# The first norm of blocks 2 and 3 taken from x by features, in a stick-breaking attention layer

## The chip, the cores and the metric

One Trainium2 chip, and one of its cores: TensorE (PE in the profile, its weight loads PEld), VectorE (DVE), ScalarE (ACT), GpSimd (POOL), and the DMA queue that SyncE (SP) issues. The metric is the device time of one execution in microseconds. It is given as the median of several runs, and less is better.

## The reference, cut to what matters

One encoder layer on 2048 tokens of 1024 features, all float32: adaptive norm, stick-breaking attention with 16 heads, a gated residual, then a second norm and a dense SwiGLU. The change touches the first line alone.

```python
h = modulate(rms_norm(x, norm_g[i, 0]), sh_m, sc_m)   # h * (1 + scale) + shift, per feature
y = stick_breaking_mixer(h, sb_w_qkv[r], sb_w_o[r])   # qkv = h @ w_qkv, blocks of causal attention, @ w_o
x = x + gt_m * rms_norm(y, norm_g[i, 1])
h = modulate(rms_norm(x, norm_g[i, 2]), sh_f, sc_f)
x = x + gt_f * rms_norm(swiglu_ffn(h, ffn_w_in[i], ffn_w_out[i]), norm_g[i, 3])

def rms_norm(x, g):                                   # over the 1024 features of a token
    return x * lax.rsqrt(jnp.mean(x * x, axis=-1, keepdims=True) + EPS) * g
```

## The kernel before, in words

The tokens are cut into four blocks of 512 (numbered 0 to 3), the features into eight tiles of 128 (k = 0 to 7), the heads into eight pairs (p). Products want h with the features on the partitions: per tile, 128 x 512. A product in full precision is made of three matmuls with high and low halves (`mm3`, L172 to L176), so each tile of h is kept as a high half in fp32r and a low half that is the rest. These are the tiles `ht`.

The order on TensorE, ScalarE, VectorE and GpSimd is the order in which the code is written (a manual schedule; SP's order alone is chosen by the scheduler). Each of these queues works strictly in that order, so an instruction that waits holds up everything behind it.

`project` (L446) makes K, then Q, then V of one pair and block, eight k-steps each. They are called t = 1, 0 and 2, and their accumulators in PSUM `pj`. As pair 0 works on block b - 1, the first norm of block b (`nb` in the code) is put between its k-steps, at places that are written as (t, k). Attention units (scores `z`, sigmoids, the scan `w`, the product `a`, turns `t`, halves `aT`, the weighing `o`) are interleaved with these steps from the V product of block 1 on.

Before the change the first norm is done in two ways:

- Blocks 1 and 3 "by features" (`BY_FEATURES`, L73): x is loaded twice, by tokens (`x`, four tiles of 128 x 1024) for the sums of squares, and by features (`xc`, four tiles with two k each) for the values. ScalarE squares each token tile with a running sum (L165), VectorE and GpSimd make 1/rms of it (L167, L169), VectorE spreads it over 128 columns (L340), TensorE turns the four spread pieces into a row over all 512 tokens (`xr`, L352), ScalarE copies that to SBUF. VectorE (even k) or GpSimd (odd k) then multiply the feature tiles by this row (L372, L376); ScalarE makes the high half (L389, or L394 and L395), VectorE or GpSimd the low one (L390, L397).
- Block 2 by tokens: x is loaded once; after the same sums VectorE scales the token tiles (L338), and TensorE turns each k with four transposes (`xT`, L361). ScalarE applies gain and shift as it reads PSUM (`hf`, L383), VectorE makes both halves (L384, L385).

`NORM_AT` (L75) places the tiles k = 0, 1, 2 of the next block inside the V product before it; the tiles k = 3 to 7 are made inside the K product that uses them, at its k-steps 0 to 4.

Of the kernel before, what the change touches and what calls it, by code (L numbers as in the profile page):

```python
# [9 lines left out]
F32 = mybir.dt.float32  # L10
# [59 lines left out]

H2_STEP = 3

BY_FEATURES = (1, 3)  # L73

NORM_AT = [(2, 2), (2, 4), (2, 6)]  # L75

# [26 lines left out]
def hybrid_trunk_kernel(  # L103
# [183 lines left out]


    x_tiles, x_norm, x_rstd, x_cols, x_row = {}, {}, {}, {}, {}

    x_places = {}

    def x_place(b):
        if b not in x_places:
            x_places[b] = [
                att.tile([P, 2, D], F32, name=f"x{b}_{i}", tag="qt", bufs=BUFS["qt"]) for i in range(2)
            ]
        return x_places[b]

    def x_load(b, *which):  # L300
        for i in which or range(4):
            r0 = b * BT + i * P
            if b == 2:
                tok = x_place(b)[i // 2][:, i % 2]
            else:
                tok = att.tile([P, D], F32, name=f"x{b}_{i}", tag="v", bufs=BUFS["v"])
            nc.sync.dma_start(tok, x[r0 : r0 + P])
            x_tiles[b, i] = tok

    def cols_load(b, *which):  # L310
        for m in which or range(KC // 2):
            cols = att.tile([P, 2, BT], F32, name=f"xc{b}_{m}", tag="kt", bufs=BUFS["kt"])
            nc.sync.dma_start(cols, xt[b // 2, :, 2 * m : 2 * m + 2])
            x_cols[b, 2 * m], x_cols[b, 2 * m + 1] = cols[:, 0], cols[:, 1]

    def x_square(b, i):
        if b > 0:
            tok = x_tiles[b, i]
            if b in BY_FEATURES:
                junk = tok  # L320
            else:
                junk = att.tile([P, D], F32, name=f"xj{b}_{i}", tag="wraw", bufs=BUFS["wraw"])
            x_rstd[b, i] = rms_scale(att, tok, f"n0_{b}_{i}", junk=junk)
            return
        xn = att.tile([P, D], F32, name=f"xn{b}_{i}", tag="kt", bufs=BUFS["kt"])
        x_norm[b, i] = xn
        x_rstd[b, i] = rms_scale(att, x_tiles[b, i], f"n0_{b}_{i}", junk=xn)

    def x_scale(b, i):
        nc.vector.tensor_scalar(  # L330
            x_norm[b, i], x_tiles.pop((b, i)), x_rstd.pop((b, i)), None, op0=ALU.mult
        )

    def x_spread(b, i):

        if b not in BY_FEATURES:
            tok = x_norm[b, i] = x_tiles.pop((b, i))
            nc.vector.tensor_scalar(tok, tok, x_rstd.pop((b, i)), None, op0=ALU.mult)  # L338
            return
        nc.vector.tensor_scalar(  # L340
            x_tiles[b, i][:, :P], ones, x_rstd.pop((b, i)), None, op0=ALU.mult
        )

    def x_share(b):

        if b not in BY_FEATURES:
            return
        pool, tag = (tps, "t") if b < 2 else (accps, "acc")
        pt = pool.tile([P, BT], F32, name=f"xr{b}", tag=tag)
        for i in range(4):  # L350
            tok = x_tiles.pop((b, i))
            nc.tensor.transpose(pt[:, i * P : (i + 1) * P], tok[:, :P], ident)  # L352
        x_row[b] = tok[:, BT:]
        nc.scalar.copy(x_row[b], pt)

    def x_turn(b, k):

        pool, tag = (tps, "t") if b == 0 else (accps, "acc")
        pt = pool.tile([P, BT], F32, name=f"xT{b}_{k}", tag=tag)
        for i in range(4):  # L360
            nc.tensor.transpose(  # L361
                pt[:, i * P : (i + 1) * P], x_norm[b, i][:, k * P : (k + 1) * P], ident
            )
        return pt

    def scale_cols(b, k):

        if b not in BY_FEATURES:
            return
        u = x_cols[b, k]  # L370
        if k % 2 == 0 or b == 1:
            nc.vector.scalar_tensor_tensor(  # L372
                u, u, g_eff[:, 0, k : k + 1], x_row[b], op0=ALU.mult, op1=ALU.mult
            )
        else:
            nc.gpsimd.tensor_tensor(u, u, x_row[b], op=ALU.mult)  # L376

    def modulate(hl, b, k):

        gain, add = g_eff[:, 0, k : k + 1], mod[:, 0, k : k + 1]  # L380
        if b not in BY_FEATURES:
# [4 lines left out]
            return  # L386
        u = x_cols.pop((b, k))
        if k % 2 == 0 or b == 1:
            nc.scalar.activation(hl[:, 0], u, AF.Identity, bias=add)  # L389
# [56 lines left out]
    def project(at):  # L446
# [10 lines left out]
        def product(t):  # L457
# [7 lines left out]
            for k in range(KC):  # L465
                if t == 1:
                    if p == 0:
                        first_norm(b, k + (4 if b == 1 else 3))
                    if k == 0 and nb == 3:
                        cols_load(3)  # L470
                    if k in (3, 5) and waiting:
                        waiting.pop(0)()
                if nb == 2 and (t, k) == (0, 0):
                    x_load(3)
                square_at = {2: 0, 3: 1}.get(nb)
                if t == square_at and k < 4:
# [12 lines left out]
                yield  # L489
# [260 lines left out]
            )  # L750

    def turn_x(m):
        turned_x[m] = x_turn(0, m)

    def full(m):
        t = att.tile([P, BT], F32, name=f"hf0_{m}", tag="tmp", bufs=BUFS["tmp"])
# [26 lines left out]
    nc.sync.dma_start(c_act, c)  # L783
    row_load(0)
    nc.sync.dma_start(c_line[0:1], c_row)
    x_load(0)
    nc.sync.dma_start(b_cols, ada_b_cols)
    nc.sync.dma_start(gc, g_cols)
    row_load(1)
# [21 lines left out]
    row_done(0)  # L811
    for i in range(1, 4):
        x_square(0, i)
        x_scale(0, i - 1)
    for half in range(2):
        nc.scalar.copy(c_rows[:, half * BT : (half + 1) * BT], c_spread[half])
    x_scale(0, 3)
    row_load(6)
    row_load(7)
    first_acc = {  # L820
# [44 lines left out]
    low(2)  # L865
    products(1, 0, 2)
    products(1, 1, 2)
    for m in range(3):
        cols_load(1, m)
    store(0)  # L870
    x_load(1, 0, 1, 2)
    row_done(3)
    full(3)
    high(3)
# [24 lines left out]
    products(0, 4)  # L899
    products(1, 4)  # L900
    turn_x(7)
    x_place(2)
    store(2)
    x_load(2)
    cols_load(1, 3)
    full(6)
    high(6)
# [2 lines left out]
    row_done(7)  # L910
    low(6)
    x_square(1, 0)
    products(0, 5)
    products(1, 5)
    full(7)
# [842 lines left out]
```

## Time and profile before

| | us |
|---|---|
| median of 3 runs (lowest, highest) | 2849.67 (2843.75, 2851.95) |
| the profiled execution's own time | 2845.32 |
| its span in the trace | 2843.2 |
| TensorE busy in it | 2800.4 (98%) |
| VectorE, ScalarE, GpSimd busy | 2021.7, 1634.1, 1282.5 |

TensorE is busy in nearly all of the span. What it waits for is small and lies mostly in the first 150 us, where the first norm, the first projections and the first attention units of pair 0 run together. A timeline row gives the start in us from the span's start, the busy time, the engine, the line, the operation, and in brackets how long the engine sat idle before and what ended that. Rows of matmuls overlap: a 128x512 matmul is busy for 0.39 us, and the next one starts 0.23 us after it.

### The profile page before, as it was taken

To read this page: it belongs to the slowest core of one execution; us is meant where nothing else is said; L and a number is where in the kernel's file an instruction comes from. 1 tells how busy PE (TensorE), PEld (TensorE's weight loads), DVE (VectorE), ACT (ScalarE), POOL (GpSimd) and SP (SyncE) were. 2 spreads that over 40 slices of the span, in tenths; PEclk is the share of its full clock that TensorE was granted. 3 is DMA by queue.
4 is the path that set the end of the run, shared out by engine and by line. 5 is a ranking of instruction groups with operands and counts; after the bars stand their busy time and mean duration, and the time that the engine had idled before them with its cause. 6 is when DMAs were issued, how large, how long until landed. Compare 5 with 4: busy or idle time off the path is not lost.

```text
span 2843.2 us, 41829 instructions
## 1 busy us (share of the span) xinstructions
PE 2800.4 (98%) x13853; PEld 2338.5 (82%) x13853; DVE 2021.7 (71%) x2822; ACT 1634.1 (57%) x3274; POOL 1282.5 (45%) x2032
## 2 busy tenths in 40 slices
PE   9899999999999999999999999999999999999998
PEld 7788888888888888887888788888788888888887
DVE  6788888888888888888866766555775655134377
ACT  5787778787777877778645533333433333322243
POOL 0565666676576655666410122222222222544454
PEclk9999999999999999999999999999999999999999
DMA  9774556666665635546389644334453335545575
GB/s 368 285 230 157 186 170 212 211 188 216 196 217 177 218 116 175 193 136 228 97 293 317 196 139 153 120 103 160 127 176 110 112 105 166 191 138 153 181 227 187
DMA packets 239787, 521.05 MB, mean 183 GB/s; under 512 B 22481, under 2 KB 108497, under 8 KB 222674
## 3 DMA queue, kind: packets, MB, share of 16 engines
q1 hardware_dynamic: 239570, 518.38, 56.4%
q8 instruction: 109, 1.79, 0.3%
q14 instruction: 108, 0.88, 0.1%
HBM read 351.04 MB, written 118.49 MB: 165 GB/s over the span
## 4 chain that ended last, share of the span: by engine, by line
PE 84%; DVE 5%; DMA 5%; ACT 2%; issue 2%; POOL 1%; SPq 0%; DVEq 0%; POOLq 0%; ACTq 0%
PE s L174 9%; PE s L175 9%; PE s L176 9%; PE z L593 8%; PE o L672 8%; PE t L644 8%; PE pj L174 5%; PE pj L176 5%; PE pj L175 5%; PE o L176 4%; PE o L174 4%; PE o L175 4%; DMA h_s<-ht 1%; PE y L176 1%; PE y L174 1%
## 5 line engine op out<-in xcount | busy, mean ns | idle before, releaser
L634 POOL TENSOR_TENSOR a<-a,w 128x512 f32<-128x512 f32 (+3 forms) x640 | 621.6, 971 | 217.2 <-DVE w L627 130.3
L627 DVE TENSOR_TENSOR_SCAN w<-z,c,begin 128x512 f32<-128x512 f32 x384 | 489.3, 1278 | 83.9 <-ACT z L612 60.6
L174 PE MATMUL s<-r,l 128*128 128x512 f32 x1232 | 482.3, 391 | 5.1 <-DVE p L1490 3.9
L176 PE MATMUL s<-r,l 128*128 128x512 f32 x1232 | 480.2, 390 | 0.0
L175 PE MATMUL s<-r,l 128*128 128x512 f32 x1232 | 479.9, 390 | 0.0
L610 ACT ACTIVATE a<-z 128x512 f32<-128x512 f32 (+3 forms) x640 | 347.1, 542 | 170.4 <-PE z L593 137.6
L672 PE MATMUL o<-aT,v 128*128 128x512 f32 (+3 forms) x1280 | 385.0, 382 | 0.1
L660 DVE TENSOR_TENSOR aT<-t,aT 128x512 fp32r<-128x512 f32 (+3 forms) x640 | 358.6, 594 | 23.9 <-ACT aT L654 23.4
L593 PE MATMUL z<-kt,qt 128*128 128x512 f32 (+3 forms) x1280 | 363.7, 365 | 0.0
L654 ACT CAST aT<-t 128x512 fp32r<-128x512 f32 (+3 forms) x640 | 313.9, 533 | 73.5 <-PE t L644 63.4
L612 ACT ACTIVATE z<-z 128x512 f32<-128x512 f32 (+3 forms) x640 | 344.8, 539 | 0.0
L1498 POOL TENSOR_TENSOR one<-p,p 128x512 f32<-128x512 f32 x44 | 70.9, 1612 | 579.1 <-issue 322.2
L174 PE MATMUL pj<-ht,w 128*128 128x512 f32 x768 | 308.4, 402 | 4.3 <-issue 1.4
L644 PE MATMUL t<-begin,a 128*128 128x128 f32 x2176 | 295.7, 274 | 13.8 <-DVE aT L660 12.5
L644 PEld LDWEIGHTS t<-begin,a 128*128 128x128 f32 x2176 | 255.7, 141 | 64.1 <-DVE aT L660 14.0
L175 PE MATMUL pj<-ht,w 128*128 128x512 f32 x768 | 301.5, 393 | 2.0 <-DVE ht L390 1.5
L176 PE MATMUL pj<-ht,w 128*128 128x512 f32 x768 | 301.9, 393 | 0.0
L174 PEld LDWEIGHTS s<-r,l 128*128 128x128 f32 x1232 | 231.7, 188 | 56.0 <-ACT l L1351 2.9
L176 PEld LDWEIGHTS s<-r,l 128*128 128x128 f32 x1232 | 231.5, 188 | 48.3
L175 PEld LDWEIGHTS s<-r,l 128*128 128x128 f32 x1232 | 231.7, 188 | 48.0 <-issue 0.5
L622 DVE TENSOR_TENSOR_SCAN w<-z,begin 128x128 f32<-128x128 f32 (+3 forms) x256 | 208.6, 817 | 76.7 <-ACT z L612 67.5
L593 PEld LDWEIGHTS z<-kt,qt 128*128 128x128 f32 x1280 | 231.0, 189 | 37.6 <-DVE w L622 0.2
(178 smaller groups left out, 4879.3 us busy)
## 6 DMA issues: line engine op xcount, KB each, us to landing
ht<-h_s SPq DMA_DIRECT2D x108, 1024.0 KB, 8.2
wi<-in_win SPq DMA_DIRECT2D x86, 512.0 KB, 4.0
qt<-qn SPq DMA_DIRECT2D x124, 256.0 KB, 4.8
ol_qt<-act_s SPq DMA_DIRECT2D x56, 512.0 KB, 3.7
act_s<-S SPq DMA_DIRECT2D x66, 256.0 KB, 4.1
br<-in_wout SPq DMA_DIRECT2D x66, 256.0 KB, 3.5
h_s<-ht SPq DMA_DIRECT2D x16, 1024.0 KB, 9.8
o_s<-os SPq DMA_DIRECT2D x128, 128.0 KB, 2.6
```

Of the source, the lines that this page charges most:

```text
L174: nc.tensor.matmul(acc, lhs[0], rhs[0], start=first, stop=False, **kw)
L175: nc.tensor.matmul(acc, lhs[0], rhs[1], start=False, stop=False, **kw)
L176: nc.tensor.matmul(acc, lhs[1], rhs[0], start=False, stop=last, **kw)
L593: nc.tensor.matmul(z[:, :n], q[:, e, part, r * P : (r + 1) * P], k[:, e, :n], start=part == 0, stop=part == 1,)
L610: nc.scalar.activation(a[:, :n], z[:, :n], AF.Sigmoid, scale=QK_SCALE)
L612: nc.scalar.activation(z[:, :n], z[:, :n], AF.Sigmoid, scale=-QK_SCALE)
L627: nc.vector.tensor_tensor_scan(rest[:, rev], left[:, rev], begin[:, :BT][:, rev], initial=carries[r], op0=ALU.mult, op1=ALU.bypass,)
L634: nc.gpsimd.tensor_tensor(a[:, :n], a[:, :n], rest[:, 1 : n + 1], op=ALU.mult)
L644: nc.tensor.transpose(pt[:, rb * P : (rb + 1) * P], weighed[i, rb][:, j * P : (j + 1) * P], ident)
L654: nc.scalar.copy(hl[:, 0, t0:], pt[:, t0:])
L660: nc.vector.tensor_tensor(hl[:, 1, t0:], pt[:, t0:], f32(hl[:, 0, t0:]), op=ALU.subtract)
L672: nc.tensor.matmul(acc[:, t0:], lhs, hl[:, part, t0:], start=sc == qb and j == 0 and part == 0, stop=sc == 0 and j == 3 and part == 1,)
```

## The change

Blocks 1 to 3 are now all treated by features, and the token tiles of blocks 2 and 3 are no longer loaded.

- Sums of squares of blocks 2 and 3 come from the feature tiles: ScalarE squares each `xc` tile (two k, 1024 elements a partition) into `xs`; VectorE adds these to one tile, first by pairs of k (three additions of 1024 elements), then its two halves (512 elements). Four matmuls with a column of ones (`xq`, one column of output each) sum over the partitions, so 128 tokens land on the partitions of each column. VectorE and GpSimd make 1/rms for all four columns at once (`xm`, `xd`), VectorE spreads it into `xw`, and TensorE turns that into the row `xr`, which ScalarE copies to `xv`, as before for blocks 1 and 3.
- Block 2's squares use two tiles, so that ScalarE can fill one while VectorE adds the other. Block 3's four squares use one tile: the third and the fourth go to the half whose content VectorE has just added.
- Block 2 loses its 32 transposes, the scaling of its token tiles and `hf`; its odd k are multiplied on GpSimd and take two passes on ScalarE, as block 3's.
- The places are written in three tables: `XSQUARE_AT`, `XADD_AT` and `XSUM_AT` (for the summing matmuls, the spread and the turn). Each (t, k) stands before that k-step of the block before.
- The row and the spread pieces get tiles of their own in the pool "tmp". The constant `lead` holds -0.5 for the power.

```diff
-BY_FEATURES = (1, 3)
+XSQUARE_AT = {2: {(1, 2): 0, (1, 3): 1, (1, 6): 2, (1, 7): 3}, 3: {(1, 4): 0, (1, 5): 1, (0, 0): 2, (0, 2): 3}}
+XADD_AT = {2: {(1, 5): 1, (1, 7): 2, (0, 0): 3, (0, 1): 4}, 3: {(1, 7): 1, (0, 1): 2, (0, 3): 3, (0, 4): 4}}
+XSUM_AT = {2: [(0, 2), (0, 3), (0, 5)], 3: [(0, 5), (0, 6), (0, 7)]}
...
-    nc.vector.memset(lead, 0.0)
+    nc.vector.memset(lead, -0.5)
...
+    def cols_square(b, m):
+        if m == 0 or (m == 2 and b == 2):
+            both = att.tile([P, 2, 2, BT], F32, name=f"xs{b}_{m}", tag="qt", bufs=BUFS["qt"])
+            x_squares.setdefault(b, []).extend([both[:, 0], both[:, 1]])
+        elif m > 1 and b == 3:
+            x_squares[b].append(x_squares[b][1])
+        nc.scalar.activation(x_squares[b][m], x_pairs.pop((b, m)), AF.Square)
+
+    def cols_add(b, m):
+        total = x_squares[b][0]
+        if m < KC // 2:
+            nc.vector.tensor_tensor(total, total, x_squares[b][m], op=ALU.add)
+        else:
+            nc.vector.tensor_tensor(total[:, 0], total[:, 0], total[:, 1], op=ALU.add)
+
+    def cols_sum(b):
+        total = x_squares.pop(b)[0]
+        ps = accps.tile([P, BT], F32, name=f"xq{b}", tag="acc")
+        for i in range(4):
+            nc.tensor.matmul(
+                ps[:, i : i + 1], total[:, 0, i * P : (i + 1) * P], ones[:, 0:1], start=True, stop=True
+            )
...
+        nc.vector.tensor_scalar(ms, ps[:, :4], 1.0 / D, EPS, op0=ALU.mult, op1=ALU.add)
...
+        nc.gpsimd.tensor_tensor(rstd, ms, lead[:, :4], op=ALU.pow)
...
     def modulate(hl, b, k):
...
-        if b not in BY_FEATURES:
-            u = att.tile([P, BT], F32, name=f"hf{b}_{k}", tag="tmp", bufs=BUFS["tmp"])
-            nc.scalar.activation(u, x_turn(b, k), AF.Identity, bias=add, scale=gain)
-            nc.vector.tensor_copy(hl[:, 0], u)
-            nc.vector.tensor_tensor(hl[:, 1], u, f32(hl[:, 0]), op=ALU.subtract)
-            return
...
-                    if k == 0 and nb == 3:
-                        cols_load(3)
...
-                if nb == 2 and (t, k) == (0, 0):
-                    x_load(3)
-                square_at = {2: 0, 3: 1}.get(nb)
-                if t == square_at and k < 4:
-                    x_square(nb, k)
-                if t == square_at and 2 <= k < 6:
-                    x_spread(nb, k - 2)
-                if nb and (t, k) == (0, 1):
-                    x_share(nb)
+                if nb == 2 and (t, k) == (1, 4):
+                    cols_load(3)
+                if nb:
+                    if (t, k) in XSQUARE_AT[nb]:
+                        cols_square(nb, XSQUARE_AT[nb][t, k])
+                    if (t, k) in XADD_AT[nb]:
+                        cols_add(nb, XADD_AT[nb][t, k])
+                    if (t, k) in XSUM_AT[nb]:
+                        (cols_sum, x_spread, x_share)[XSUM_AT[nb].index((t, k))](nb)
...
-    x_load(2)
+    cols_load(2, 0, tag="v")
     cols_load(1, 3)
...
+    cols_load(2, 1, 2, tag="v")
...
+    cols_load(2, 3, tag="v")
```

VectorE, at block 1's K and Q products: the first norm of block 2, before. A name's last number is that of its buffer: `n_2_0_ssq` is the sum of squares of block 2's first 128 tokens, `x_0_531` holds two token tiles, `kn_1_745` the halves of block 1's K.

```order
L496 TENSOR_TENSOR kn_1_745<-pj_1_1_689,kn_1_745 128x512
L167 TENSOR_SCALAR n_2_0_ms<-n_2_0_ssq 128x1
L167 TENSOR_SCALAR n_2_1_ms<-n_2_1_ssq 128x1
L167 TENSOR_SCALAR n_2_2_ms<-n_2_2_ssq 128x1
L338 TENSOR_SCALAR x_0_531<-x_0_531,n_2_0_rstd 128x1024
```

And the same place now (`xs_0` and `xs_2` the tiles of squares, `xq` the sums in PSUM, `xm` and `xd` the mean and 1/rms, `xw` the spread pieces):

```order
L326 TENSOR_TENSOR xs_0_711<-xs_0_711 128x1024
L326 TENSOR_TENSOR xs_0_711<-xs_0_711,xs_2_755 128x1024
L491 TENSOR_TENSOR kn_1_765<-pj_1_1_693,kn_1_765 128x512
L326 TENSOR_TENSOR xs_0_711<-xs_0_711,xs_2_755 128x1024
L328 TENSOR_TENSOR xs_0_711<-xs_0_711 128x512
L338 TENSOR_SCALAR xm_787<-xq_782 128x4
L348 TENSOR_SCALAR xw_794<-ones,xd_789 128x128 x4
```

The last addition has to be done before TensorE's summing matmuls, which stand ahead of k-step 2 of block 1's Q product.

ScalarE, at the end of block 2's K product and the start of its Q product, before (`x_3_760` the last token tile of block 3, `xT_7` the last turned tile of block 2, the rest attention):

```order
L165 ACTIVATE x_3_760,n_3_3_ssq<-x_3_760 128x1024
L383 ACTIVATE hf_7_1031<-xT_7_1032,mod,g_eff 128x512
L610 ACTIVATE a_1_1046<-z_1_1008 128x256
L612 ACTIVATE z_1_1008<-z_1_1008 128x256
L610 ACTIVATE a_2_1072<-z_2_1052 128x384
L612 ACTIVATE z_2_1052<-z_2_1052 128x384
L654 CAST aT_0_1078<-t_0_1062 128x512
```

And now (`xs_0_966` block 3's one tile of squares):

```order
L321 ACTIVATE xs_0_966<-xc_0_731 128x1024
L605 ACTIVATE a_1_972<-z_1_953 128x256
L607 ACTIVATE z_1_953<-z_1_953 128x256
L321 ACTIVATE xs_0_966<-xc_1_733 128x1024
L605 ACTIVATE a_2_998<-z_2_978 128x384
L607 ACTIVATE z_2_978<-z_2_978 128x384
L649 CAST aT_0_1004<-t_0_988 128x512
L490 CAST kn_2_1014<-pj_2_1_912 128x512
L321 ACTIVATE xs_0_966<-xc_2_735 128x1024
L649 CAST aT_1_1027<-t_1_993 128x384
```

The squares of block 3 stood ahead of block 2's last tiles; now they stand behind them, among the first attention units.

VectorE, in block 2's Q product now (`xs_0_966` again block 3's squares), where before only the attention rows stood:

```order
L491 TENSOR_TENSOR kn_2_1014<-pj_2_1_912,kn_2_1014 128x512
L655 TENSOR_TENSOR aT_1_1027<-t_1_993,aT_1_1027 128x384
L617 SCALAR_TENSOR_TENSOR w_3_1030<-z_3_1007,begin 128x512
L326 TENSOR_TENSOR xs_0_966<-xs_0_966 128x1024
L617 SCALAR_TENSOR_TENSOR w_0_1053<-z_0_1037,begin 128x128
L655 TENSOR_TENSOR aT_2_1062<-t_2_1048,aT_2_1062 128x256
L326 TENSOR_TENSOR xs_0_966<-xs_0_966 128x1024
L328 TENSOR_TENSOR xs_0_966<-xs_0_966 128x512
```

Block 3's additions of the third and the fourth square now stand between the scans and halves of the attention; the first one stands ahead of `kn_2`.

More of the change, by code (lines that the diff above doesn't have):

```diff
@@ L289, in hybrid_trunk_kernel @@
     x_tiles, x_norm, x_rstd, x_cols, x_row = {}, {}, {}, {}, {}
[L291 to L308, printed above, removed]
@@ L326, in x_square @@
[L326 to L334, printed above, removed]
-        if b not in BY_FEATURES:
[L337 to L342, printed above, removed]
+        junk = x_tiles[b, i]
@@ L344, in x_share, with x_spread @@
+    def x_spread(b, *which):
+        if b not in x_spreads:
+            x_spreads[b] = att.tile([P, 4, P], F32, name=f"xw{b}", tag="tmp", bufs=BUFS["tmp"])
+        for i in which or range(4):
+            rstd = x_rstd[b][:, i : i + 1] if b > 1 else x_rstd.pop((b, i))
+            nc.vector.tensor_scalar(x_spreads[b][:, i], ones, rstd, None, op0=ALU.mult)
     def x_share(b):
-        if b not in BY_FEATURES:
-            return
+        spread = x_spreads.pop(b)
         pool, tag = (tps, "t") if b < 2 else (accps, "acc")
@@ L785, in hybrid_trunk_kernel @@
     nc.sync.dma_start(c_line[0:1], c_row)
-    x_load(0)
+    for i in range(4):
+        x_load(0, i)
     nc.sync.dma_start(b_cols, ada_b_cols)
@@ L813, in hybrid_trunk_kernel @@
         x_square(0, i)
-        x_scale(0, i - 1)
+        x_scale(i - 1)
     for half in range(2):
         nc.scalar.copy(c_rows[:, half * BT : (half + 1) * BT], c_spread[half])
-    x_scale(0, 3)
+    x_scale(3)
     row_load(6)
@@ L867, in hybrid_trunk_kernel @@
     products(1, 1, 2)
-    for m in range(3):
-        cols_load(1, m)
+    cols_load(1, 0, 1, 2)
     store(0)
-    x_load(1, 0, 1, 2)
+    for i in range(3):
+        x_load(1, i)
     row_done(3)
```

50 lines of the change are left out of this document (25 added, 25 removed).

## The prediction

> **What bounds the kernel now.** I read the page's first lines, then what TensorE waited for, then windows over the stretch in which the first norms are made.
>
> ```profile
> span 2843.2 us, 41829 instructions
> PE 2800.4 (98%) x13853; PEld 2338.5 (82%) x13853; DVE 2021.7 (71%) x2822; ACT 1634.1 (57%) x3274; POOL 1282.5 (45%) x2032
> ```
>
> TensorE is busy for 98% of the span. Work of another engine costs time only where TensorE waits for it; TensorE work that goes, or a wait that comes, moves the end by its own length. The waits of TensorE in the first 150 us are next (in all, times, longest):
>
> ```profile
> PE t L644 <- DVE aT L660: 6.0, 4, 2.3
> PE xT L361 <- DVE x L338: 1.5, 3, 0.7
> PE pj L175 <- DVE ht L390: 1.5, 1, 1.5
> ```
>
> All three are waits for VectorE, whose rows the change makes more, not fewer. The windows (engine busy, then granted clock and DMA):
>
> ```profile
> 77.30:80.70 3.40, 1.87 (x8) 1.32 (x9) 2.69 (x5) 1.04 (x2) 1.23 (x3) 1.00 1.01 419
> 80.70:84.10 3.40, 3.40 (x13) 2.80 (x12) 1.95 (x4) 1.11 (x3) 0.00 (x0) 0.50 0.99 391
> 88.60:100.10 11.50, 10.70 (x57) 7.93 (x56) 11.05 (x24) 11.11 (x23) 5.70 (x13) 1.00 1.00 369
> 121.70:125.10 3.40, 1.10 (x8) 0.78 (x6) 3.40 (x4) 2.07 (x7) 3.01 (x4) 1.00 0.56 231
> 125.10:128.50 3.40, 3.40 (x16) 3.27 (x15) 2.61 (x7) 2.10 (x5) 2.42 (x8) 0.50 0.48 154
> ```
>
> Block 2's K product (88.6 to 100.1) has VectorE and ScalarE full, 11.05 and 11.11 of 11.50. And twice a window in which TensorE was busy for 1.87 or 1.10 of 3.40 us is followed by one at a granted clock of 0.50, which costs up to half of 3.40, 1.7 us. So a stall costs more than its length.
>
> **The change part by part.** Everything that it touches lies before 130 us. TensorE's starts in block 1's Q, block 1's V, block 2's K and Q:
>
> ```profile
> 71.22 0.39 PE L174 MATMUL pj<-ht,w 128*128 128x512 f32 x1
> 75.30 0.39 PE L174 MATMUL pj<-ht,w 128*128 128x512 f32 x1
> 76.96 0.33 PE L361 MATMUL xT<-begin,x 128*128 128x128 f32 x1
> 79.57 0.47 PE L174 MATMUL pj<-ht,w 128*128 128x512 f32 x1
> 81.29 1.05 PE L361 MATMUL xT<-begin,x 128*128 128x128 f32 x4
> 82.00 0.77 PE L174 MATMUL pj<-ht,w 128*128 128x512 f32 x1
> 88.21 0.60 PE L361 MATMUL xT<-begin,x 128*128 128x128 f32 x4
> 88.56 0.48 PE L174 MATMUL pj<-ht,w 128*128 128x512 f32 x1
> 100.13 0.39 PE L174 MATMUL pj<-ht,w 128*128 128x512 f32 x1
> 105.93 0.40 PE L174 MATMUL pj<-ht,w 128*128 128x512 f32 x1
> 109.47 0.39 PE L174 MATMUL pj<-ht,w 128*128 128x512 f32 x1
> 25.91 1.84 PE L708 MATMUL acol<-c_act,ar 128*128 128x1 f32 x16
> ```
>
> They are: Q k-step 2 of block 1 at 71.22, V of block 1 at 75.30, the first turn (76.96) to the k-step behind it (79.57), a turn of tile k = 1 (81.29 to 82.00), one of the later turns (88.21 to 88.56), Q of block 2 at 100.13, its k-step 5 at 105.93, its V at 109.47.
>
> *1. Block 2's sums, a new wait.* The summing matmuls stand ahead of Q k-step 2 (71.22). They need ScalarE's four squares and VectorE's four additions, and both engines are still at block 1's last tiles then:
>
> ```profile
> 65.89 0.72 ACT L389 ACTIVATE ht<-xc,mod 128x512 fp32r<-128x512 f32 x1 [1.99 <-DVE xc L372]
> 67.84 1.05 ACT L545 CAST v<-vt 128x512 fp32r<-128x512 f32 x2
> 70.10 0.59 ACT L495 CAST kn<-pj 128x512 fp32r<-128x512 f32 x1 [1.20 <-issue]
> 67.10 2.07 DVE L390 SCALAR_TENSOR_TENSOR ht<-xc,mod,ht 128x512 fp32r<-128x512 f32 x3
> 69.09 1.28 DVE L546 TENSOR_TENSOR v<-vt,v 128x512 fp32r<-128x512 f32 x2
> L165 ACT ACTIVATE xj<-x 128x1024 f32<-128x1024 f32 x4 | 4.2, 1052 | 2.0 <-DMA k_park<-kn 2.0
> L742 DVE TENSOR_TENSOR w<-wr,w 128x1024 fp32r<-128x1024 f32 x6 | 7.3, 1223 | 1.5 <-ACT w L738 1.5
> L338 DVE TENSOR_SCALAR x<-x,n_rstd 128x1024 f32<-128x1024 f32 x4 | 2.9, 745 | 0.1
> ```
>
> A square goes by L165's row: 1.05 us, less 0.08 by which rows overlap (three of L390 take 2.07, so one starts every 0.66). An addition of 1024 elements goes by L742, 1.22 (1.14 apart). ScalarE after 65.89 has the high halves of k = 6 and 7, two casts of v, kn and four squares, nine rows: it ends at 72.5, at least. VectorE can begin its second v addition only at about 70.1, since a square stands before ScalarE's second v cast. Then come additions 1 and 2 (to 73.0), kn (0.6), addition 3 (to 74.7), the halves (L546 has 0.64 for one) to 75.5. TensorE would be there at 71.22: a stall of 4.3. VectorE's row alone (69.09 + 1.28 + 0.6 + 3 x 1.14 + 0.65 = 75.0) gives 3.8, so its length does not hang on ScalarE's order. Even if an addition of float32 took the 0.75 of L338, which reads one tile and not two, 2.4 would be left.
>
> The four one-column matmuls cost 4 x 0.115 = 0.5 by L708's row. The turn of `xw` costs 0.35 (88.21 to 88.56), and a last wait for power and spread 0.2 (0 to 1.2; four k-steps lie between). Together **+5.35**: V of block 1 starts at 80.65.
>
> *2. Block 2 no longer turned.* Eight turns go: 2.61 (with the waits for L338) + 0.71 (81.29 to 82.00) + 6 x 0.35 = 5.42. TensorE's idle 0.80 in 88.6 to 100.1 can go as well, and the half-clock window behind the first turn (80.7 to 84.1) costs 1.7, less 0.35 that the turn in it already counts, 1.35. That is 7.57 of the 24.83 us from 75.30 to 100.13. So TensorE alone could end block 2's K at 80.65 + 17.26 = 97.9. But the odd tiles now go over GpSimd's multiplication and two passes on ScalarE:
>
> ```profile
> L376 POOL TENSOR_TENSOR xc<-xc,x 128x512 f32<-128x512 f32 x4 | 6.0, 1505 | 0.0
> 114.39 1.37 DVE L390 SCALAR_TENSOR_TENSOR ht<-xc,mod,ht 128x512 fp32r<-128x512 f32 x1
> ```
>
> GpSimd takes 1.5 a tile, and VectorE's L390 took 1.37 beside it where it takes 0.69 alone. I add 2.0 for this (0 to 3.1), so K ends at 99.9 (97.9 to 101): from 80.65 on 5.6 is won back, and the net up to here is **-0.2** (-2.2 to +0.9).
>
> *3. Block 3's sums, a second new wait.* Before, its token squares lay ahead of block 2's last tiles. Now squares and additions follow each other through one tile, with attention rows between them on both queues:
>
> ```profile
> L169 POOL TENSOR_TENSOR n_rstd<-n_ms,mhalf 128x1 f32<-128x1 f32 x16 | 11.5, 719 | 70.1 <-DVE n_ms L167 69.9
> L622 DVE TENSOR_TENSOR_SCAN w<-z,begin 128x512 f32<-128x512 f32 x4 | 4.9, 1220 | 0.9 <-ACT z L612 0.9
> L622 DVE TENSOR_TENSOR_SCAN w<-z,begin 128x384 f32<-128x384 f32 x5 | 4.8, 955 | 3.1 <-ACT z L612 3.0
> L610 ACT ACTIVATE a<-z 128x512 f32<-128x512 f32 x13 | 7.8, 602 | 0.1
> L610 ACT ACTIVATE a<-z 128x384 f32<-128x384 f32 x5 | 2.6, 514 | 2.1 <-PE z L593 2.1
> L660 DVE TENSOR_TENSOR aT<-t,aT 128x512 fp32r<-128x512 f32 x10 | 6.7, 674 | 1.6 <-ACT aT L654 1.6
> ```
>
> I count from block 2's last high half on ScalarE, about 1.4 before K ends. First leg: two squares with two activations of 256 between (1.0 + 0.6 + 1.0), two of 384 (0.9), the scan of 384 on VectorE (0.95), its aT (0.6), addition 1 (1.1): about 6.0. Second: square 3 may write only now (1.05), aT and two activations of 512 (1.4), the scan of 512 (1.2), addition 2 (1.15): to 10.8. Third: square 4 (1.1), activation, scan and aT of the short pieces (1.0), addition 3 (1.15), the halves (0.65): to 14.7, or 13.3 after K ends. TensorE's own work from K's end to the place (k-step 5) is 105.93 - 100.13 - 0.4 for a wait of before = 5.4. So it waits about 7.9, partly already at the attention's turns. The rest, 0.46 for the sums, 3.54 to V (105.93 to 109.47), 0.35 and 0.2, as above: V starts 17.85 after K's end instead of 9.34, **+8.5**. The least that I can make of it, with additions of 0.75 and no other row of the attention in the way, is +4; the most, with each of VectorE's additions held as L390 was at 114.39, is +11.
>
> Sum of 1 to 3: -0.2 + 8.5 = **+8.3**. Two long stalls bring one to three half-clock windows where one goes: +2.0 by the windows above (1 to 3), so **+10.3**.
>
> [...]
>
> *4. Edits at nothing.* Own tiles for the row and its pieces, and `lead`, add no row. The queue that SP issues moves:
>
> ```profile
> 76.01 6.28 SPq L512 DMA_DIRECT2D kt<-kn  x4
> 94.64 3.55 SPq L528 DMA_DIRECT2D qt<-qn  x4
> ```
>
> Block 3's four feature tiles (0.5 MB each, 5.0 us at 419 GB/s) now stand ahead of such loads, and block 1's K and Q pieces come later by that; the first unit that reads them follows after 100 us, so some 15 us cover it (uncovered: up to 5.0). Block 2's and 3's token tiles, 4 MB, are no longer loaded; nothing waited for them but L338 and L165's 2.0 us for a tile, both counted.
>
> **The rivals.** *A, the stalls pay themselves back.* While TensorE waits for the sums, ScalarE and VectorE catch up with the attention, and the 6.0 us of L644's waits in 100 to 150, their half-clock window (125.1 to 128.5, 1.7) and the added ones (2.0) go: 10.3 - 9.7 = +0.6, 2850.3. It decides from about 6 us of work that VectorE can do ahead. Against it: VectorE is what L644 waits for, it was full already (11.05 of 11.50), and gets 2 x 4 us of additions in the same stretch.
>
> *B, only block 2's wait is real*, because the attention rows between block 3's additions wait for TensorE anyway: steps 1 and 2 remain, with the clock's part and the sums' 0.8 for block 3: +0.4 to +2, 2851. Against it: the third square can't start before the first addition, which stands behind a scan.
>
> *C, neither wait comes*, as block 1's own tiles arrive earlier because less is loaded: -7.57 + 2 x 0.5 + 0.35 = -6.2, 2843.5. It needs VectorE 4.3 us earlier at 69. Against it: ScalarE waited for VectorE there (1.99), not for a DMA.
>
> *D, more of the same*: the odd tiles on GpSimd hold VectorE in all of block 2's K (up to +3), block 3's chain at its long end (+2.5) and two more half-clock windows (3.4): +14 to +20, 2866.
>
> That the change does nothing of this sort is excluded by the order: the additions stand there.
>
> **How the numbers follow.** The profiled execution took 2845.32; +10.3 makes 2855.6. The median is 4.35 above that execution, so against the median 2849.67 + 10.3 = **2860.0**. About 0.3%, 8.5 us, can be told from no change: slower means above 2858.2, faster below 2841.1. The forecast with its bounds (+5 to +16) has 0.60, of which 0.44 is slower and 0.16 the same. A has 0.14 (0.02 faster, 0.12 same), B 0.10 (same), C 0.06 (0.04 faster, 0.02 same), D 0.10 (slower). That is 0.06 faster, 0.40 same, 0.54 slower. The range 2847 to 2868 leaves out C, the lower part of A and the upper half of D, with some 0.05 of the forecast's own ends.
>
> **What would show it.** Right: TensorE waiting some 4 us for VectorE's last addition at the first summing matmul near 71 to 76, V of block 1 at about 80.6, no turns and full clock up to about 100, block 2's Q still starting near 100; then some 8 us of waits before the second summing matmul, V of block 2 near 118 instead of 109.47, and from there the same distance to the end. Wrong: a summing matmul that waits less than 2 us, a Q of block 2 before 97 or behind 102, L644's waits in 100 to 150 well below 6.0, or a shift that grows or shrinks behind 150.

## The result, and the profile after

The changed kernel takes 2864.68 us (median; 2861.50 to 2871.13), the kernel before 2850.02 beside it (2843.75 to 2853.15). The ratio is 1.0056, with a 95% interval from 1.0036 to 1.0077: slower by 0.56%, or 14.7 us by the medians. Forecast were +10.3 and slower, in a range from 2847 to 2868.

The page of the changed kernel, first lines, and TensorE's waits from 60 to 170 us, which holds the work that before does in its first 150 us:

```profile
span 2867.2 us, 41789 instructions
PE 2815.9 (98%) x13841; PEld 2351.6 (82%) x13841; DVE 2021.5 (71%) x2820; ACT 1635.7 (57%) x3271; POOL 1283.3 (45%) x2030
```

```profile
PE t L639 <- DVE aT L655: 8.1, 5, 2.6
PE xq L334 <- DVE xs L328: 7.2, 2, 4.4
PE pj L179 <- DVE ht L387: 3.9, 2, 2.3
```

The second row is new: TensorE waits twice at the summing matmuls, 7.2 us in all. The other two are the old kinds. The waits for the attention's halves have grown from 6.0 in four to 8.1 in five (a new one of 2.58, and 5.5 in the four of before), those for block 1's and block 2's tiles from 1.5 to 3.9.

The two profiled executions differ by 24 us of span, and 9.8 of these arise ahead of the last turn of block 0, where TensorE does the same work in both. So I count from that turn to a mark behind everything that was changed, the wait of 1.15 for one and the same half of the attention. Before, then after, on TensorE's timeline:

```profile
48.25 0.60 PE L361 MATMUL xT<-begin,xn 128*128 128x128 f32 x4
139.31 0.55 PE L644 MATMUL t<-begin,a 128*128 128x128 f32 x3 [1.15 <-DVE aT L660]
```

```profile
58.06 0.60 PE L366 MATMUL xT<-begin,xn 128*128 128x128 f32 x4
164.02 0.55 PE L639 MATMUL t<-begin,a 128*128 128x128 f32 x3 [1.15 <-DVE aT L655]
```

It is 91.06 before and 105.96 after: **+14.9**, which agrees with the medians. Spans less the first mark differ by 14.2 (2809.1 and 2795.0), so nearly nothing is added or won back later. Between the marks lie the places of the prediction:

```profile
80.80 0.39 PE L180 MATMUL pj<-ht,w 128*128 128x512 f32 x1
85.59 1.86 PE L334 MATMUL xq<-ones,xs 128*128 128x1 f32 x8 [4.40 <-DVE xs L328]
87.31 0.77 PE L178 MATMUL pj<-ht,w 128*128 128x512 f32 x1
91.30 0.75 PE L355 MATMUL xr<-begin,xw 128*128 128x128 f32 x4
91.80 0.48 PE L178 MATMUL pj<-ht,w 128*128 128x512 f32 x1
93.97 0.39 PE L178 MATMUL pj<-ht,w 128*128 128x512 f32 x1
108.26 0.50 PE L179 MATMUL pj<-ht,w 128*128 128x512 f32 x1 [2.33 <-DVE ht L387]
114.09 0.39 PE L178 MATMUL pj<-ht,w 128*128 128x512 f32 x1
119.36 0.48 PE L639 MATMUL t<-begin,a 128*128 128x128 f32 x1 [2.58 <-DVE aT L655]
126.61 1.86 PE L334 MATMUL xq<-ones,xs 128*128 128x1 f32 x8 [2.79 <-DVE xs L328]
128.34 0.77 PE L178 MATMUL pj<-ht,w 128*128 128x512 f32 x1
134.52 0.51 PE L178 MATMUL pj<-ht,w 128*128 128x512 f32 x1
```

From the first mark, V of block 1 starts at 35.9 (93.97; before 27.05), Q of block 2 at 56.0 (114.09; before 51.9), V of block 2 at 76.5 (134.52; before 61.2): first +8.9, then -4.7, then +11.1. The windows show what comes with the waits (columns: PE busy, PEld, DVE, ACT, POOL, then the granted clock):

```profile
81.00:84.40 3.40, 0.19 (x1) 0.00 (x0) 3.30 (x4) 1.27 (x2) 0.00 (x0) 1.00 1.04 429
84.40:88.20 3.80, 2.61 (x10) 2.52 (x11) 1.26 (x3) 0.00 (x0) 0.47 (x1) 0.55 1.01 420
88.20:91.60 3.40, 3.40 (x10) 2.52 (x10) 0.88 (x4) 0.00 (x0) 0.54 (x1) 0.50 1.03 419
105.40:108.80 3.40, 1.05 (x3) 0.69 (x4) 3.40 (x4) 2.41 (x5) 2.85 (x4) 0.98 1.03 346
108.80:112.20 3.40, 3.40 (x10) 2.47 (x10) 2.88 (x4) 2.80 (x5) 1.38 (x4) 0.52 0.99 419
120.30:122.20 1.90, 1.90 (x7) 1.51 (x6) 1.84 (x2) 0.00 (x0) 1.02 (x1) 0.50 0.27 61
122.20:126.60 4.40, 1.63 (x8) 1.16 (x6) 2.85 (x5) 3.20 (x9) 1.52 (x5) 0.89 0.00 0
128.30:131.70 3.40, 3.40 (x11) 2.71 (x12) 1.90 (x6) 0.00 (x0) 1.15 (x3) 0.50 0.03 7
```

Behind each of the four waits of 4.40, 2.33, 2.58 and 2.79 stands a stretch at half clock (granted 0.50 to 0.55), and the work right behind the wait runs in it: the summing matmuls, the nine matmuls up to the turn of the row, the turns of the attention.

### The profile page after: what moved, and what is told of

It is laid out like the page before. It is cut to its first block, busy times and chain, and to the rows that moved or that the text cites. A ratio compares the mean times of both kernels' runs of the same rounds, so it can differ in the third digit from the quotient of the medians.

```text
span 2867.2 us, 41789 instructions
## 1 busy us (share of the span) xinstructions
PE 2815.9 (98%) x13841; PEld 2351.6 (82%) x13841; DVE 2021.5 (71%) x2820; ACT 1635.7 (57%) x3271; POOL 1283.3 (45%) x2030
## 4 chain that ended last, share of the span: by engine, by line
PE 85%; DVE 4%; ACT 2%; issue 2%; DMA 1%; POOL 1%; DVEq 0%; SPq 0%; POOLq 0%; ACTq 0%
PE s L178 9%; PE s L179 9%; PE s L180 9%; PE z L588 8%; PE o L667 8%; PE t L639 8%; PE pj L178 5%; PE pj L180 5%; PE pj L179 5%; PE o L180 4%; PE o L178 4%; PE o L179 4%; PE y L180 1%; PE y L178 1%; PE y L179 1%
## 5 line engine op out<-in xcount | busy, mean ns | idle before, releaser
L622 DVE TENSOR_TENSOR_SCAN w<-z,c,begin 128x512 f32<-128x512 f32 x384 | 489.1, 1278 | 84.2 <-ACT z L607 61.9
L639 PE MATMUL t<-begin,a 128*128 128x128 f32 x2176 | 296.9, 274 | 16.0 <-DVE aT L655 14.7
L617 DVE TENSOR_TENSOR_SCAN w<-z,begin 128x128 f32<-128x128 f32 (+3 forms) x256 | 208.7, 817 | 78.2 <-ACT z L607 67.2
```

The costliest lines, as they stand in the source:

```text
L622: nc.vector.tensor_tensor_scan(rest[:, rev], left[:, rev], begin[:, :BT][:, rev], initial=carries[r], op0=ALU.mult, op1=ALU.bypass,)
L639: nc.tensor.transpose(pt[:, rb * P : (rb + 1) * P], weighed[i, rb][:, j * P : (j + 1) * P], ident)
```

## The experiments

All against before on the same chip. "V1", "Q2" and "V2" are the starts of V of block 1, Q of block 2 and V of block 2 from the first mark, "behind" is the second mark less 91.06. "Earlier" is the same difference at an earlier mark, the attention's wait of 2.2 to 2.3 us that before has at 124.23 (75.98 from its first mark).

| run | ratio (95% interval) | V1 | Q2 | V2 | behind | earlier |
|---|---|---|---|---|---|---|
| before | 1 | 27.1 | 51.9 | 61.2 | 0 | 0 |
| the change | 1.0056 (1.0036 to 1.0077) | 35.9 | 56.0 | 76.5 | +14.9 | +14.9 |
| e1_late2 | 1.0048 (1.0035 to 1.0062) | 29.2 | 52.2 | 72.5 | +11.1 | +11.0 |
| e2_free | 1.0028 (1.0016 to 1.0039) | 33.5 | 54.7 | 70.7 | +8.1 | +9.1 |
| e3_tok3 | 1.0016 (1.0004 to 1.0027) | 36.8 | 57.9 | 67.2 | +6.0 | +5.9 |
| e4_tok3_late2 | 0.9999 (0.9989 to 1.0009) | 30.0 | 54.3 | 63.7 | +1.3 | +2.3 |
| f1_two3 | 1.0035 (1.0021 to 1.0049) | 35.4 | 57.3 | 74.2 | +11.6 | +12.7 |
| f4_late3 | 1.0058 (1.0043 to 1.0072) | 35.3 | 57.1 | - | +14.1 | +14.1 |
| f2_dve2 | 1.0050 (1.0033 to 1.0067) | 35.4 | 55.4 | 75.0 | +13.5 | +13.5 |
| f3_tok3_late2_dve2 | 0.9998 (0.9987 to 1.0008) | 29.6 | 53.7 | 63.1 | +0.9 | +1.9 |
| g3_noadd3 | 1.0014 (1.0004 to 1.0024) | 35.4 | 55.4 | 67.1 | +4.6 | +5.6 |
| g2_both_mended | 1.0022 (1.0008 to 1.0035) | 29.5 | 51.5 | 68.2 | +6.6 | +6.6 |
| g1_tok3_spread_dve2 | 0.9995 (0.9985 to 1.0005) | 29.5 | 54.1 | 63.4 | +1.2 | +2.2 |

Times and marks tell the same story: 0.1% is 2.85 us, and no run's ratio stands more than 3 us from its mark "behind".

The two last columns differ by 1.0 in six runs, for a reason that no edit made. From the wait of 2.2 to 2.3 to the next one it takes 8.7 to 8.8 us in before, the change, e1, e3, f2, f4 and g2, and 7.7 in e2, e4, f1, f3, g1 and g3. In before and in the change the granted clock over it is 0.80, in before 0.50 from 125.10 to 128.50; the eight turns that lie in it take 1.91 in before (from 126.37) and 1.28 in f1_two3 (from 141.63). Here before, then f1_two3:

```profile
124.23 0.33 PE L644 MATMUL t<-begin,a 128*128 128x128 f32 x1 [2.30 <-DVE aT L660]
132.93 0.63 PE L644 MATMUL t<-begin,a 128*128 128x128 f32 x4 [0.85 <-DVE aT L660]
```

```profile
139.72 0.33 PE L639 MATMUL t<-begin,a 128*128 128x128 f32 x1 [2.27 <-DVE aT L655]
147.40 0.63 PE L639 MATMUL t<-begin,a 128*128 128x128 f32 x4 [0.84 <-DVE aT L655]
```

So the same wait brings a stretch at half clock in some executions and none in others, and "earlier" is the fairer column. Single marks scatter too: the change, f1_two3 and f4_late3 have the same TensorE work up to Q2, and their V1 stands at 35.3 to 35.9, their Q2 at 56.0 to 57.3. Each run has one profile, so differences of about 1 us between two runs say nothing.

**The place of block 2's sum.**

```diff
-XSUM_AT = {2: [(0, 2), (0, 3), (0, 5)], ...
+XSUM_AT = {2: [(0, 7), (2, 0), (2, 1)], ...
```

> Block 2's summing matmuls, spread and turn later: ahead of Q's k-step 7 and V's k-steps 0 and 1 (now k-steps 2, 3 and 5 of Q); nothing else is changed. Marks are counted from the last turn of block 0 (xT<-xn), since the two profiled executions differ by 9.8 us ahead of it: before has V of block 1 at 27.05, Q of block 2 at 51.88, V of block 2 at 61.22; the changed kernel 35.9, 56.0 and 76.5. Theory W (what costs is the place at which TensorE waits for the sums, and the half clock behind it): the wait of 4.4 shrinks to about 1, no half-clock window follows, V of block 1 at 29 to 30.5, Q of block 2 at 51 to 53, and 3 to 5 us less than the changed kernel in all (ratio to before about 1.004). Rival L (what costs is the added load on VectorE, ScalarE and GpSimd; TensorE would wait for a later tile instead): V of block 1 earlier, but Q of block 2 still at 55 to 56, and at most 1 us less (1.0055).

On its timeline of TensorE, the wait of 4.40 is 0.99, the eight matmuls take 1.05 and not the 1.86 that they take at a granted clock of 0.50 in the change, and the turn has a wait of its own:

```profile
85.96 1.05 PE L334 MATMUL xq<-ones,xs 128*128 128x1 f32 x8 [0.99 <-DVE xs L328]
89.55 0.83 PE L355 MATMUL xr<-begin,xw 128*128 128x128 f32 x4 [1.04 <-DVE xw L348]
```

V1 comes 6.7 earlier, Q2 3.8, and at the second mark 3.8 of it are left, as theory W had it. The ratio, 1.0048, agrees with that but does not prove it, as the intervals overlap.

**Sums that wait for nothing.**

```diff
+        src = [ones] * 4 if b in (2, 3) else [total[:, 0, i * P : (i + 1) * P] for i in range(4)]
...
-                ps[:, i : i + 1], total[:, 0, i * P : (i + 1) * P], ones[:, 0:1], start=True, stop=True
+                ps[:, i : i + 1], src[i], ones[:, 0:1], start=True, stop=True
```

> The summing matmuls of both blocks read the constant ones instead of the sums of squares; squares, additions and all else stay, only their result is not used (the output is not the reference's). So TensorE cannot wait for squares, at unchanged load of the other engines. Theory W: both waits at the sums (4.4 and 2.8) go with their half-clock windows; V of block 1 at 28.5, Q of block 2 at 50 to 53, V of block 2 at 64 to 70, 7 to 11 us less than the changed kernel (ratio to before 1.0015 to 1.003). Rival L: the waits turn up at the tiles of block 2 and at the attention's turns, Q of block 2 at 55, V of block 2 at 74 or later, at most 3 us less.

6.8 less than the change by the marks (5.8 by the earlier one), under theory W's 7 to 11, though its ratio lies in W's, and V1 not at 28.5 but at 33.5. The wait went only one step on:

```profile
84.22 1.06 PE L356 MATMUL xr<-begin,xw 128*128 128x128 f32 x4 [2.89 <-DVE xw L349]
```

The spread `xw` stands in VectorE's queue behind the additions, so the turn waits for the additions although the sums do not. In block 3 the waits moved on as well, in part to the attention's turns as rival L had it: 1.53 and 1.59 for halves and 1.56 at the turn of the row stand in the place of 2.58 and 2.79. W is right on the wait and was too simple on where it can be taken away; Q2 (54.7) is rival L's 55.

**Block 3 as before.** Block 2 alone is changed; block 3's token tiles, squares, spread and turn stand where they stood.

```diff
+                if nb == 2 and (t, k) == (0, 0):
+                    for i in range(4):
+                        x_load(3, i)
+                if nb == 3 and t == 1 and k < 4:
+                    x_square(3, k)
...
-                if nb:
+                if nb == 2:
                     if (t, k) in XSQUARE_AT[nb]:
```

> Only block 2 takes the change; block 3's sums come again from token tiles (squares in block 2's K k-steps 0 to 3, spread in 2 to 5, turn ahead of Q's k-step 1, as before). Theory W: V of block 1 at 35.9 and Q of block 2 at 56.0 as in the changed kernel, give or take 1, and from there V of block 2 follows after 9.3 to 11 as before instead of 20.4: about 10 us less than the changed kernel, 3 to 5 more than before (ratio 1.0015). Rival L (block 2's late tiles make the attention late, whatever block 3 does): V of block 2 still 15 or more behind Q, at most 5 us less.

From Q2 to V2 it takes 9.4, as before (9.3), against 20.4 in the change. 8.9 of the 14.9 go, a little less than theory W's 10, and 6.0 stay with block 2 (Q2 at 57.9 is later than W's 56.0). So the loss has two parts; that they add is shown by the next run.

**Both**, the later sum and block 3 as before:

> The two edits before together: block 2 alone by features with its sum late, block 3 by token tiles. Theory W: V of block 1 at 29 to 30.5, Q of block 2 at 50.5 to 53, V of block 2 at 60 to 63: within 3 us of before (ratio 0.999 to 1.001); if GpSimd's path does not bound block 2's K, up to 4 us under it. Rival L: Q of block 2 at 55, as slow as with the sum early, ratio 1.0015.

By the time the loss is gone (0.9999, give or take 2.9 us); by the marks 1.3 to 2.3 of the 14.9 are left, so the gains of 3.8 and 8.9 add. But Q2 is at 54.3, later than in before and than theory W's 50.5 to 53, though all turns of block 2 are gone and V1 is late by only 2.9. What the turns took of TensorE was hardly worth anything; the reason is below.

**More tiles for block 3's squares.**

```diff
         elif m > 1 and b == 3:
-            x_squares[b].append(x_squares[b][1])
+            x_squares[b].append(att.tile([P, 2, BT], F32, name=f"xs{b}_{m}", tag="v", bufs=BUFS["v"]))
```

> Block 3's third and fourth square get tiles of their own; places, additions and sums stay. Marks from the last turn of block 0; the changed kernel has Q of block 2 at 56.0, V of block 2 at 76.5, waits 2.58 for the attention's half and 2.79 at block 3's sums. Theory W (ScalarE's squares and VectorE's additions take turns through one tile, and the attention stands in between): the third square starts some 2.2 earlier, the wait of 2.58 falls to about 1, that at the sums to under 0.7, V of block 2 at 70.5 to 73, 3.5 to 6 us less than the changed kernel (ratio to before 1.0035 to 1.0043). Rival Q (VectorE's own row of scans, halves and additions sets it, whatever ScalarE does): at most 1 us less.

3.3 less (2.3 by the earlier mark), between the two theories: the wait of 2.58 is 0.48, but that at the sums is still 2.33. VectorE's timeline in it, from the scan to the halves, shows why:

```profile
111.57 1.22 DVE L617 TENSOR_TENSOR_SCAN w<-z,begin 128x512 f32<-128x512 f32 x1
112.71 1.20 DVE L326 TENSOR_TENSOR xs<-xs,xs 128x1024 f32<-128x1024 f32 x1
113.83 0.41 DVE L617 TENSOR_TENSOR_SCAN w<-z,begin 128x128 f32<-128x128 f32 x1
114.16 0.40 DVE L655 TENSOR_TENSOR aT<-t,aT 128x256 fp32r<-128x256 f32 x1
114.47 1.47 DVE L326 TENSOR_TENSOR xs<-xs,xs 128x1024 f32<-128x1024 f32 x1
115.97 0.92 DVE L328 TENSOR_TENSOR xs<-xs 128x512 f32<-128x512 f32 x1
```

No row has a wait. ScalarE no longer holds it up; what is left is VectorE's own work.

**The place of block 3's sum.**

```diff
-XSUM_AT = {..., 3: [(0, 5), (0, 6), (0, 7)]}
+XSUM_AT = {..., 3: [(2, 0), (2, 1), (2, 2)]}
```

> Block 3's summing matmuls, spread and turn ahead of V's k-steps 0, 1 and 2 instead of Q's 5, 6 and 7; one tile for the squares as in the changed kernel. Theory W: the wait of 2.79 at the sums and the half clock behind it go (the 2.58 for the attention's half, ahead of it, stays); V of block 2's first own matmul can't be compared, since the sums stand inside V now, but behind V 3 to 5 us less than the changed kernel (1.0038 to 1.0045). Rival: block 3's first tiles come too late for its K then, and TensorE waits there for what it saved: under 1.5 us less.

Theory W fails here. The sums wait no more, but only 0.8 is won by the marks, which is within their scatter, and nothing by the time (1.0058). That is the rival's size, but not its cause. In the place of the wait:

```profile
120.74 0.63 PE L639 MATMUL t<-begin,a 128*128 128x128 f32 x4 [0.74 <-DVE aT L655]
122.95 0.55 PE L639 MATMUL t<-begin,a 128*128 128x128 f32 x3 [1.58 <-DVE aT L655]
```

The attention's halves stand behind the additions in VectorE's queue. Block 2 has no attention row between its additions, so there a later sum helps; in block 3 it does not.

**Block 3 without its additions.** The three additions of 1024 elements are left out, nothing else is moved.

```diff
+        if b == 3 and m < KC // 2:
+            return
         if m < KC // 2:
```

> Block 3's three additions of 1024 elements are left out of the changed kernel; its squares, the addition of the two halves (of the first square alone), the sums and their places stay (the output is not the reference's). The run f4_late3 had no wait at block 3's sums any more and gained 0.8 only: waits of 0.74 and 1.58 for the attention's halves stood in its place. Theory Q (VectorE's additions, which stand in its queue ahead of scans and halves, are what block 3's part costs): the waits at the sums and at the halves near them go, V of block 2 at 66 to 69 (76.5 in the changed kernel), 6 to 9 us less in all, about as much as with token tiles (8.9): ratio 1.0020 to 1.0030. Rival S (ScalarE's four squares, ahead of sigmoids and casts, cost as much): at most 4 us less, as with two tiles more for the squares (3.3).

10.3 less (9.3 by the earlier mark), a little over theory Q's range and about what token tiles save (8.9 and 9.0); the ratios, 1.0014 and 1.0016, agree. The two waits of 2.58 and 2.79 are 0.42 and 0.40:

```profile
106.62 0.33 PE L641 MATMUL t<-begin,a 128*128 128x128 f32 x1 [0.42 <-DVE aT L657]
110.12 1.05 PE L336 MATMUL xq<-ones,xs 128*128 128x1 f32 x8 [0.40 <-DVE xs L330]
```

So block 3's part is, in the main, VectorE's additions among the attention's rows. From Q2 to V2 it takes 11.7 here, 20.4 in the change and 9.4 with token tiles: 8.7 of the 11.1 go with the additions. What is left, 2.4, is all that ScalarE's four squares, the summing matmuls and the addition of the halves can cost together, and these are still there. (With one tile, the third square waits for an addition; without additions that wait is gone as well. What f1_two3 won, 2.3 to 3.3, is the share of the one tile.)

**Block 2's odd tiles on VectorE.**

```diff
-        if k % 2 == 0 or b == 1:
+        if k % 2 == 0 or b < 3:
```

> Block 2's odd tiles are multiplied on VectorE, with one pass on ScalarE (as block 1's), not on GpSimd with two; all else as in the changed kernel. In it VectorE's rows took 1.58, 1.76 and 1.59 at 106.6 to 117 while GpSimd worked, instead of 0.73, 0.69 and 1.20 alone, and TensorE waited 2.33 in block 2's K. Theory P (GpSimd's work slows VectorE's): that wait falls under 1, Q of block 2 from 56.0 to 53.5 to 54.5, 1 to 2.5 us less in all. Rival V (VectorE is the engine that is short in block 2's K, and gets four rows of 0.72 more): Q of block 2 at 56 to 58, no change to 2 us more.

1.4 less, in theory P's range but hardly more than the marks scatter, with Q2 at 55.4 and not at 53.5 to 54.5. And not for P's reason: TensorE's wait in block 2's K is 2.30, as it was, and the row of VectorE that it waits for takes 1.58, as it did, without any multiplication of tiles on GpSimd. TensorE, VectorE and GpSimd there:

```profile
103.98 0.79 PE L179 MATMUL pj<-ht,w 128*128 128x512 f32 x1 [2.30 <-DVE ht L387]
102.35 1.58 DVE L387 SCALAR_TENSOR_TENSOR ht<-xc,mod,ht 128x512 fp32r<-128x512 f32 x1
101.93 1.45 POOL L629 TENSOR_TENSOR a<-a,w 128x512 f32<-128x512 f32 x1 [2.45 <-DVE w L617]
```

It is the attention's product on GpSimd that lies beside it, and ahead of it in VectorE's queue a scan of 1.21. In the changed kernel the next row of VectorE lies beside the tile's multiplication:

```profile
106.62 1.58 DVE L387 SCALAR_TENSOR_TENSOR ht<-xc,mod,ht 128x512 fp32r<-128x512 f32 x1
108.12 1.76 DVE L394 TENSOR_TENSOR ht<-xc,ht 128x512 fp32r<-128x512 f32 x1
107.62 1.72 POOL L379 TENSOR_TENSOR xc<-xc,xv 128x512 f32<-128x512 f32 x1
```

In both, VectorE's row ends shortly after GpSimd's row beside it: the one at 102.35 of f2_dve2 0.55 after (103.93 and 103.38), the one at 108.12 of the change 0.54 after (109.88 and 109.34). Where GpSimd stood still, from 95.3 to 99.5 in the change, the same two lines took 0.75 (L387 at 96.97) and 0.69 (L394 at 98.33), so most of such a length lies behind the end of GpSimd's row. What makes VectorE's rows longer there is not shown.

**What adds up.** First the edits of e4_tok3_late2 and f2_dve2 together:

> Block 2 alone by features with the sum late (as the run e4_tok3_late2, which had Q of block 2 at 54.3 and V of block 2 at 63.7), and its odd tiles on VectorE. Theory P: Q of block 2 at 52 to 53, V at 61.5 to 62.5, 0.5 to 2 us under that run: ratio to before 0.9993 to 1.000. Rival V: Q at 54.3 or later, ratio 1.000 to 1.0007.

0.9998 and +0.9: 0.4 better than e4_tok3_late2 by either mark, under theory P's 0.5 to 2 and within the scatter, with Q2 at 53.7 and not at 52 to 53.

Then the whole change, mended (with the edits of f1_two3 and f2_dve2 beside this one):

```diff
-XSUM_AT = {2: [(0, 2), (0, 3), (0, 5)], ...
+XSUM_AT = {2: [(0, 7), (0, 7), (2, 1)], ...
```

> The whole change with what helped so far: block 2's sum and spread ahead of Q's k-step 7, its turn ahead of V's k-step 1, its odd tiles on VectorE, two tiles more for block 3's squares. If the gains add up (3.8 + 3.3 + 1.4 of 14.9 by the marks behind V of block 2, and about 1 for the earlier spread): 5 to 7 us more than before, ratio 1.0018 to 1.0025. If they overlap, since VectorE is full in block 2's K: 8 to 10 more, 1.003.

+6.6 and 1.0022: the gains add. What is left is nearly all block 3's, V2 16.7 behind Q2 where before has 9.3.

And the same places with block 3 as before:

> As the run f3_tok3_late2_dve2 (block 2 alone by features, sum late, odd tiles on VectorE; 0.9 behind before by the mark at 91), with the spread one place earlier, ahead of VectorE's half of Q. Theory: the row for block 2 comes 1.2 earlier, and VectorE, which is busy from there to the end of block 2's K, ends that much earlier: Q of block 2 at 52.3 to 53, the mark at 90.6 to 91.4, so within 0.5 us of before (ratio 0.999 to 1.0005). If VectorE's row does not bound K, no change to that run.

No gain: Q2 54.1, +1.2. The row came 0.6 earlier, but then ScalarE's first token square of block 3 waited 1.26 for its tile (0.47 in f3_tok3_late2_dve2), ahead of the last high halves of block 2:

```profile
90.05 1.06 ACT L169 ACTIVATE x<-x 128x1024 f32<-128x1024 f32 x1 [1.26 <-DMA x<-in_x]
```

It is the best by time (0.9995), but its interval and those of f3_tok3_late2_dve2 and e4_tok3_late2 hold 1. They beat the changed kernel by some 0.6%; none beats the kernel before by more than a measurement can tell.

## Why the prediction came out as it did

The direction, the places of the two new waits and what ends them, VectorE's additions, were right. The size was short, +10.3 for +14.9 by the marks, and the reasons given for what block 2 wins back were not. One sign of being wrong came: counted on the time axis of before, Q of block 2 starts at 104.3 (48.25 + 56.03), beyond the 102 that the prediction named, because V of block 1 starts at 84.2 and not at 80.65.

*Step 1*, +5.35 foreseen, +8.9 measured (+8.2 to +9.7 in the runs that leave block 2's sum where the change has it and keep its wait). The wait was 4.3 on paper and 4.40 in the trace, and it is VectorE's last addition that ends it. Two terms were too small. The sums: I took a sixteenth of a row of x16 for one of the four matmuls, but in the trace eight stand there (x8): 1.72 (85.59 to 87.31) at a granted clock of 0.50 for 0.5, and 1.05 in e1_late2. And the half clock, which I added as a lump at the end, falls right there: nine matmuls take 3.99 (87.31 to 91.30, granted clock 0.50) instead of 2.07 at 0.23 each. 4.56 from the place where the next matmul would have stood (80.80 + 0.23 = 81.03) to 85.59, + 1.72 + 1.92 + 0.50 for the turn make 8.7.

*Step 2*, -5.55 foreseen and -4.7 measured (-2.9 in f1_two3 and f4_late3, which have the same work there), net +4.2 instead of -0.2 in the main because step 1 was larger. That -4.7 lies so near is partly luck. The reason that I gave, GpSimd's path, was mostly wrong: without it the wait of 2.3 in K stays (f2_dve2), and 1.4 was its worth at most where I had added 2.0. The price of the turns themselves was the larger error, hidden by the late start. With V1 at 29.5, all turns of block 2 gone and block 3's squares behind its last tiles, block 2's K is still paced by VectorE, here in the run g2_both_mended from shortly behind the first use of the row (80.46) to near the end of K:

```profile
82.00:97.00 15.00, 11.90 (x50) 9.20 (x49) 14.77 (x21) 10.66 (x23) 4.68 (x10) 0.90 0.99 314
```

VectorE is busy for 14.77 of 15.00, TensorE for 11.90. So the 7.6 us of TensorE's time that the prediction counted for the turns, their idle time and their half clock were worth 2.9 there (22.0 from V1 to Q2 instead of 24.8), and 0.2 to 0.7 where block 3's token squares stand in K as well. The row of before that said so was in the prediction: VectorE 11.05 and ScalarE 11.11 of 11.50 in that K. I read it as a warning for what is added, and not for what is taken away.

*Step 3*, +8.5 foreseen, +11.1 measured: waits of 2.58 and 2.79 (5.4, where I had about 7.9 in waits), but the sums took 1.73 for 0.46, and what follows the waits ran at half clock (granted 0.50 from 120.30 to 122.20 and from 126.60 to 131.70). The serial chain was the right picture in its length (13.3 from K's end to the sums on paper, 12.5 from Q2 in the trace), but the one tile was only a small part of it (f1_two3: 2.3 to 3.3); most is VectorE's additions (g3_noadd3: 9.3 to 10.3 in all).

*The clock*, +2.0 in the sum, was short. The trace shows a clock of 0.50 to 0.55 behind each of the four waits of 4.40, 2.33, 2.58 and 2.79, over more than one window behind the first and the last, where I had reckoned with one to three half-clock windows in the place of one. The windows ahead of three of them differ in what TensorE was busy for: 0.19 of 3.40, 1.05 of 3.40 and 1.63 of 4.40; behind them the clock was 0.55, 0.52 and 0.50.

*The rivals.* A, waits that pay themselves back: wrong; the waits for the attention's halves are 8.1 where before has 6.0 for the same work, since VectorE has more to do there and not less. B, only block 2's wait is real: wrong, block 3 has the larger part (8.9 of 14.9). C, no wait: wrong. D, more of the same, forecast +14 to +20: in size it came closest, but by the half clock and the sums, not by the odd tiles on GpSimd (1.4 at most, f2_dve2). Edits at nothing: nothing in the trace contradicts them; no run tested SP's order by itself.

Left open: how much of the 2.3 in block 2's K is the scan of 1.21 ahead of VectorE's row and how much the length of that row beside GpSimd's. No run separated them; as an estimate from the rows, the latter can be 0.85 of it at most (VectorE's row takes 1.58 there and about 0.73 where GpSimd stands still). Open is also what decides whether a wait of 2.3 is followed by half clock.

## What to carry to other kernels

Work taken off the fullest engine was worth what the stage's own pacing engine left of it, here 2.9 of 7.6 us (g2_both_mended): read the stage's window before pricing what goes, not only what comes. A sum that was added up on an engine which others wait for cost twice, at its own consumer (a wait of 2.79) and at a row queued behind it (2.58), and moving the consumer helped only where nothing stood in that queue: 3.8 us for block 2 (e1_late2), 0.8 for block 3 (f4_late3). And a wait like the one of 2.2 to 2.3 us is to be priced with the half clock that may follow: behind that wait it came in 7 of 13 executions here and cost 1.0 us.

## What was not expected of the hardware

The two profiled executions of before and after differ by 9.8 us ahead of the last turn of block 0, with the same instructions on TensorE. It is no effect of the change: g3_noadd3, which starts as the changed kernel does, has that mark at 48.13, like before (48.25). Both start at the low rate (the first 32 one-column matmuls take 6.96 us in each). Before ran its second 32 one-column matmuls at full rate (3.78 us from 15.57, where after takes 6.83), fell back (granted clock 0.52 from 19.2 to 22.0) and had full rate from 24 us on; after had it only from about 40. Here two of the early matmuls of one and the same loop, before and after:

```profile
30.25 0.39 PE L176 MATMUL pj<-ht,w 128*128 128x512 f32 x1
```

```profile
38.45 0.63 PE L180 MATMUL pj<-ht,w 128*128 128x512 f32 x1
```

The granted clock in the windows shows 1.00 for the slow stretch as well:

```profile
24.00:40.00 16.00, 16.00 (x58) 14.36 (x59) 9.69 (x14) 7.76 (x10) 0.00 (x0) 1.00 1.03 409
```

There the length of a row (0.63 for 0.39) tells the rate, not the clock column. In the profiled executions of all runs the first mark fell between 47.97 and 58.44 us, and the executions of one kernel spread by 5 to 16 us, which is as much as this change costs: a difference between two profiles is to be counted from a mark that both have.
